# A fused diffusion block on one core: normed input for FFN 2, squares on VectorE, and a fixed distance between matmul operands

## The chip, the core and the metric

The kernel runs on one core of one Trainium2 chip. The metric is the device time of one execution in microseconds (us); smaller is better. A core has TensorE (PE in the profile; its weight loads are listed apart as PEld), VectorE (DVE), ScalarE (ACT), GpSimd (POOL) and SyncE (SP), which here issues all transfers. Each engine works through its own list of instructions in order and waits on semaphores of the others.

## The reference: what is computed

One block over 256 latent tokens and 256 context tokens, with model width 1024, in fp32:

```
x   = x   + 0.5*g1x * swiglu(modulate(rmsnorm(x), sh1x, sc1x), w13_ffn1, w2_ffn1)      # FFN 1, both streams
ctx = ctx + 0.5*g1c * swiglu(modulate(rmsnorm(ctx), sh1c, sc1c), w13_ffn1, w2_ffn1)
q,k,v,g,f,ga,gf = project(modulate(rmsnorm(...)), w_in)     # retention over 4 heads, 2-D Fourier mixing
x   = x + g2x * (sigmoid(ga)*retention_out + sigmoid(gf)*fourier) @ w_out
x   = x + 0.5*g3x * swiglu(modulate(rmsnorm(x, norm_ffn2), sh3x, sc3x), w13_ffn2, w2_ffn2)   # FFN 2, latent alone
out = rmsnorm(x, norm_final)
# rmsnorm(x, w) = x * rsqrt(mean(x*x) + eps) * w ;  modulate(h, shift, scale) = h*(1+scale) + shift
# swiglu(h, w13, w2): a, b = split(h @ w13);  (silu(a) * b) @ w2          (hidden width 2816 = 22 * 128)
```

## The kernel before

Activations lie transposed: 128 features on the partitions, tokens along the free axis, so a feature tile of the latents is 128 x 256. Every fp32 operand of a large product is held as a pair, a rounded high part and the low part that is left (names end in `h` and `l`, or the pair stands as `_0` and `_1`). `mm3` (L86) makes one product of two pairs with three matmuls into one accumulator, low weights by high input, high by low, high by high (L88, L89, L90 in every profile row). In a row such as `z<-g2h,wl` the first input is the moving operand and the second the weights. TensorE loads the weights of the following matmul while the present one streams its columns.

`load_w` (L69) fetches a weight tile with one DMA into `wr`, rounds it to `wh` on ScalarE (L78) and subtracts to `wl` on VectorE (L79; some early gate and key tiles on GpSimd). There are four buffers of each, so weights run two FFN tiles ahead.

The stages in order of time: conditioning and first products (to 66 us), FFN 1 with 512 columns (to about 400; its last two output tiles are made by stream, with 256 columns), four retention heads and the Fourier transform (`kc`, `kx`, `q`, `s`, `u`, `o`, `f`, to about 607), gates with the rest of the Fourier work (`g`, `sq`, `mx`, to 670), the merge (`gg`, `ro`, to 783), the output projection (`yo`, to 806), FFN 2 up (`fa`, `fb`, to 939), FFN 2 down (`z`, to 1003) and the final norm.

`add_sq` (L446) collects the sum of squares for a norm: ScalarE squares a feature tile into `sq` (L454), GpSimd adds it into `ssum` (L455). A matmul with a matrix of 1/1024 (`ones`) then sums over the partitions; ScalarE takes the root and VectorE the reciprocal (`rstd_of`, L222 on; the reciprocal is L228).

In FFN 2 the input `hx` is not normed: `out_proj` (L938 on) scales each feature by its column of `amul` and appends two columns, the shift vector and zeros, so a matmul streams 258 columns. Each of the 22 hidden tiles (`ffn2_up`, L966) is made with 48 matmuls (8 features, two halves `fa` and `fb`, three matmuls each); the division by the norm and the shift come afterwards, on the product: two copies of the shift columns (L978, L979), two multiplications by `rstd` (L981, L983), Silu with a bias (L982), a combined add and multiply (L984), and the split into `g2h` and `g2l`. The norm's matmul `st3` (L974) stands in the code behind the matmuls of the first hidden tile.

After the opening, which is ordered by hand, a planner sets the order of each engine's list when the kernel is built: it takes the code's instructions with its own costs and lets a matmul go ahead where it expects the operands to be there. So the order on an engine is not the order of the code.

## Time and profile before

| | |
|---|---|
| time, median of 3 runs | 1013.61 us (1013.13 to 1014.77) |
| the profiled execution: own time / span of its instructions | 1015.47 us / 1013.7 us |
| mean granted TensorE clock | 0.994 of full speed |
| PE busy, matmuls | 984.4 us (97%), x6792 |
| DVE busy | 663.9 us (65%) |
| ACT busy | 469.4 us (46%) |
| POOL busy | 62.4 us (6%), x39 |
| read from HBM | 164.70 MB, 164 GB/s over the span |

A matmul's own duration in the profile overlaps the next one's, so it tells little of the rate. What counts on a busy TensorE is the time from one start to the next, which the timeline gives. Idle time of an engine stands in brackets behind a row, with the work that ended it.

### The profile page before, as it was taken

The numbers are of one execution on the slowest core, as the hardware profiler recorded it, in microseconds if no ns is written. First come the engines' busy times: TensorE is split into PE (matmuls) and PEld (weight loads), VectorE is DVE, ScalarE is ACT, GpSimd is POOL, SyncE is SP. The second block draws the span as 40 slices with busy tenths as digits, with TensorE's granted clock in tenths as the row PEclk, the third lists the DMA queues.
The fourth block names the chain that finished last, engine by engine and source line by source line (L and its number), as shares of the span: only waits on it lengthen the run. The fifth ranks groups of instructions, "written<-read, shape, count | busy, mean of one in ns | idle before, by whom it ended". The sixth has DMA issues, their size and how long they took to land.

```text
span 1013.7 us, 16779 instructions
## 1 busy us (share of the span) xinstructions
PE 984.4 (97%) x6792; PEld 907.9 (90%) x6792; DVE 663.9 (65%) x1084; ACT 469.4 (46%) x725; POOL 62.4 (6%) x39
## 2 busy tenths in 40 slices
PE   6999999999999998999999998999999989999996
PEld 4778888888888888999999997999999989999995
DVE  7879999998334335866575538865555766676543
ACT  4454322125222423756575456754444545555541
POOL 0000000000000013000000026000000300000011
PEclk9999999999999999999999999999999999999999
DMA  8647766994322233223133434456566446656651
GB/s 337 231 176 249 235 199 212 349 402 160 104 83 75 84 112 115 64 84 125 43 126 108 158 100 150 125 185 183 181 200 187 153 161 186 185 172 182 185 174 42
DMA packets 49238, 166.84 MB, mean 165 GB/s; under 512 B 5380, under 2 KB 7044, under 8 KB 49160
## 3 DMA queue, kind: packets, MB, share of 16 engines
q1 hardware_dynamic: 49160, 165.77, 50.8%
q8 instruction: 53, 0.87, 0.3%
q14 instruction: 25, 0.20, 0.1%
HBM read 164.70 MB, written 1.05 MB: 164 GB/s over the span
## 4 chain that ended last, share of the span: by engine, by line
PE 91%; DVE 4%; ACT 2%; DMA 1%; issue 1%; POOL 0%; DVEq 0%; SPq 0%; ACTq 0%; POOLq 0%
PE y L88 4%; PE y L89 4%; PE y L90 4%; PE pa L89 3%; PE pb L89 3%; PE pa L88 3%; PE pb L88 3%; PE pb L90 3%; PE pa L90 3%; PE ro L89 2%; PE ro L90 2%; PE ro L88 2%; PE fa L89 2%; PE z L90 2%; PE z L89 2%; PE z L88 2%
## 5 line engine op out<-in xcount | busy, mean ns | idle before, releaser
L79 DVE TENSOR_TENSOR wl<-wr,wh 128x1024 fp32r<-128x1024 f32 (+1 forms) x214 | 248.8, 1164 | 202.0 <-ACT wh L78 201.2
L78 ACT CAST wh<-wr 128x1024 fp32r<-128x1024 f32 (+1 forms) x226 | 227.0, 1006 | 273.2 <-PE y L90 79.2
L191 DVE CUSTOM_DVE_ANT_0 junk<-ada,cb,sm 128x1024 bf16<-128x1024 f32 x96 | 122.9, 1280 | 5.9 <-DMA ada<-in_ada 4.4
L89 PE MATMUL y<-gl,wh 128*128 128x512 f32 (+1 forms) x198 | 72.5, 366 | 0.0
L88 PE MATMUL y<-gh,wl 128*128 128x512 f32 (+1 forms) x198 | 72.4, 366 | 0.0
L90 PE MATMUL y<-gh,wh 128*128 128x512 f32 (+1 forms) x198 | 72.3, 365 | 0.0
L455 POOL TENSOR_TENSOR ssum<-ssum,sq 128x256 f32<-128x256 f32 (+1 forms) x18 | 24.6, 1367 | 727.3 <-ACT sq L454 714.2
L89 PE MATMUL pa<-h1l,wh 128*128 128x512 f32 x152 | 59.1, 389 | 0.0
L88 PE MATMUL pa<-h1h,wl 128*128 128x512 f32 x152 | 59.1, 389 | 0.0
L90 PE MATMUL pa<-h1h,wh 128*128 128x512 f32 x152 | 59.1, 389 | 0.0
L88 PE MATMUL pb<-h1h,wl 128*128 128x512 f32 x152 | 59.1, 389 | 0.0
L89 PE MATMUL pb<-h1l,wh 128*128 128x512 f32 x152 | 59.1, 389 | 0.0
L90 PE MATMUL pb<-h1h,wh 128*128 128x512 f32 x152 | 59.1, 389 | 0.0
L89 PE MATMUL fa<-hxl,wh 128*128 128x258 f32 x176 | 50.8, 289 | 0.0
L88 PE MATMUL fa<-hxh,wl 128*128 128x258 f32 x176 | 50.8, 289 | 0.0
L90 PE MATMUL fa<-hxh,wh 128*128 128x258 f32 x176 | 50.6, 287 | 0.0
L89 PE MATMUL fb<-hxl,wh 128*128 128x258 f32 x176 | 50.1, 284 | 0.0
L89 PE MATMUL z<-g2l,wh 128*128 128x256 f32 x176 | 50.0, 284 | 0.0
L88 PE MATMUL fb<-hxh,wl 128*128 128x258 f32 x176 | 50.0, 284 | 0.0
L90 PE MATMUL fb<-hxh,wh 128*128 128x258 f32 x176 | 49.9, 283 | 0.0
L88 PE MATMUL z<-g2h,wl 128*128 128x256 f32 x176 | 49.8, 283 | 0.0
L90 PE MATMUL z<-g2h,wh 128*128 128x256 f32 x176 | 49.8, 283 | 0.0
(310 smaller groups left out, 2908.3 us busy)
## 6 DMA issues: line engine op xcount, KB each, us to landing
ada<-in_ada SPq DMA_DIRECT2D x72, 512.0 KB, 5.1
wr<-in_w13b SPq DMA_DIRECT2D x44, 512.0 KB, 4.3
wr<-in_w13a SPq DMA_DIRECT2D x38, 512.0 KB, 4.3
wrv<-in_wv SPq DMA_DIRECT2D x16, 512.0 KB, 4.3
wr<-in_wg SPq DMA_DIRECT2D x16, 512.0 KB, 4.2
wr<-in_wgate SPq DMA_DIRECT2D x16, 512.0 KB, 4.3
wr<-in_pret SPq DMA_DIRECT2D x16, 512.0 KB, 3.8
wr<-in_w2b SPq DMA_DIRECT2D x16, 512.0 KB, 3.6
```

The costliest lines, as they stand in the source:

```text
L78: S.copy(hi[:, :n], raw[:, :n])
L79: (lo_engine or V).tensor_tensor(lo[:, :n], raw[:, :n], f32(hi[:, :n]), op=ALU.subtract)
L88: PE.matmul(o, w[1], a[0], start=start, stop=False)
L89: PE.matmul(o, w[0], a[1], start=False, stop=False)
L90: PE.matmul(o, w[0], a[0], start=False, stop=stop)
L191: V.tensor_tensor_reduce(junk, raw, cb[:, s, :], 1.0, sm[:, BIAS + n : BIAS + n + 1], ALU.mult, ALU.add, mod[:, s, n : n + 1],)
L455: G.tensor_tensor(ssum[0][:, cols], ssum[0][:, cols], sq[:, :w], op=ALU.add)
```

## The change

Three things are changed.

1. FFN 2 takes a normed input from hidden tile 4 on (`RAW = 4`). Tiles 0 to 3 still use `hx` with 258 columns. While they run, `modulated` makes `hn`, the normed, scaled and shifted input, for the eight features: on VectorE one instruction for `xr`, on ScalarE one for `hnh`, on VectorE one for `hnl`. Tiles 4 to 21 stream 256 columns of `hn`; behind them stand only Silu from the accumulator, one multiplication and the split. The norm's matmul moves behind the first half of tile 1, and tiles 0 and 1 are finished together.
2. In `add_sq` the addition into `ssum` is on VectorE instead of GpSimd: five additions of 512 columns and thirteen of 256.
3. Small pads shift tiles in SBUF. Each pad is a tile that VectorE sets to zero once, nine in all, of 8 to 120 columns; `at=16` shifts some weights within their buffer, and `hx` tiles are rounded up to 288 columns.

What the third does to the layout can be told with one number for each matmul: the address of the next matmul's weights minus that of this matmul's moving operand, in bytes within 512. Here are these distances as the two built programs have them, leaving out the few matmuls at a change of stage.

| matmuls | count | before | changed |
|---|---|---|---|
| FFN 1 `pa`, `pb`, `y`, 512 columns | 1374 | 256 | 256 |
| FFN 1 last two output tiles, `y`, 256 columns | 132 | 256 | 320 |
| heads: `kc`, `kx`, `q`, `o`, and gates `g` | 1536 | 320 | 320 |
| heads: `s` and `u` | 480 | 0 | 320 |
| Fourier `f`, 512 columns | 96 | 192 | 192 |
| Fourier `sq`, `mx` | 96 | 0 | 320 |
| merge: `gg`, `ro` | 960 | 320 | 320 |
| output projection `yo` | 192 | 256 | 320 |
| FFN 2 up, tiles 0 to 3, 258 columns | 192 | sixteen values, 0 to 480 in steps of 32 | 96, 224, 352, 480 |
| FFN 2 up, tiles 4 to 21 | 864 | the same sixteen, 258 columns | 320, 256 columns |
| FFN 2 down `z` | 528 | 256 | 320 |

A distance of 320 means that the moving operand stands 192 bytes behind the weights, within 512.

The planner's order changes at three places. On PE, around the norm's matmul of FFN 2, it stood before the change between the first products of tile 0 (names end in the tile's number, then a buffer number):

```order
L88 MATMUL fa0_8180<-hxh6_7855,wl160_8190 128x258
L88 MATMUL fb0_8181<-hxh6_7855,wl160_8190 128x258
L974 MATMUL st3_8179<-ssum3_7859,ones_90 128x256
L88 MATMUL fa1_8259<-hxh0_7843,wl161_8263 128x258
L89 MATMUL fa1_8259<-hxl0_7844,wh161_8262 128x258
```

and now:

```order
L97 MATMUL fb0_8219<-hxh7_7875,wh160_8227 128x258
L96 MATMUL fa1_8280<-hxl7_7876,wh162_8289 128x258
L97 MATMUL fa1_8280<-hxh7_7875,wh162_8289 128x258
L987 MATMUL st3_8318<-ssum3_7879,ones_90 128x256
L95 MATMUL fb1_8281<-hxh0_7861,wl161_8284 128x258
L96 MATMUL fb1_8281<-hxl0_7862,wh161_8283 128x258
```

It moved from place 39 among FFN 2's matmuls to place 73, behind all of tile 0 and the first half of tile 1. It no longer stands ahead of work that could run.

On DVE, behind the norm's reciprocal in FFN 2, the weights' low parts (`wl`), the raw tiles' evacuation (`a2`) and the new `xr3` and `hnl` share the list. Before:

```order
L228 RECIPROCAL rstd3_8245<-sd3_8243 128x256
L978 COPY cc0_8247<-fa0_8180 128x1
L979 COPY cc0_8247<-fb0_8181 128x1
L981 TENSOR_TENSOR a2_0_8250<-fa0_8180,rstd3_8245 128x256
L983 TENSOR_TENSOR a2_0_8250<-fb0_8181,rstd3_8245 128x256
L978 COPY cc1_8321<-fa1_8259 128x1
L981 TENSOR_TENSOR a2_1_8324<-fa1_8259,rstd3_8245 128x256
```

and now, the last rows of the stretch, in which `hnl7` ends the making of the normed input:

```order
L328 SCALAR_TENSOR_TENSOR xr3_7_8536<-xs3_112,amul_104,rstd3_8322 128x256
L91 TENSOR_TENSOR g2l2_8459<-a2_2_8453,g2h2_8458 128x256
L1010 TENSOR_TENSOR a2_3_8543<-fa3_8462,rstd3_8322 128x256
L1012 TENSOR_TENSOR a2_3_8543<-fb3_8463,rstd3_8322 128x256
L86 TENSOR_TENSOR wl171_8694<-wr171_8692,wh171_8693 128x1024
L332 SCALAR_TENSOR_TENSOR hnl6_8215<-xr3_6_8532,mod_103,hnh6_8214 128x256
L86 TENSOR_TENSOR wl172_8700<-wr172_8698,wh172_8699 128x1024
L332 SCALAR_TENSOR_TENSOR hnl7_8217<-xr3_7_8536,mod_103,hnh7_8216 128x256
```

From the reciprocal to `hnl7`, which counts, there stand 8 `wl`, 11 TENSOR_TENSOR of 256 columns, 19 SCALAR_TENSOR_TENSOR of 256 and 5 COPY of one column. On PE the first matmul that reads `hnl0` is the 122nd behind `st3`, the first that reads `hnl7` the 232nd; tiles 4, 5 and 6 are interleaved there, by the feature that is ready. SP's list of transfers is the same in both.

The third place is where stage 2 begins, on DVE, between the last `xs` of FFN 1 and the first `h2cl`:

```order
L467 SCALAR_TENSOR_TENSOR xs3_112<-y1_7_1_3300,gate_105,xs3_112 128x256
L64 MEMSET pad_kt 128x48
L64 MEMSET pad_qt 128x80
L64 MEMSET pad_pt 128x80
L64 MEMSET pad_ht 128x48
L332 SCALAR_TENSOR_TENSOR h2cl0_3343<-xr2_0_0_3422,mod_103,h2ch0_3342 128x256
```

The four pads are new here; none of them waits for anything.

The diff:

```diff
--- before.py
+++ after.py
@@ -24,9 +24,11 @@
 M1 = 3
 HALF = MT // 2
 T2K = 4
+RAW = 4
 OUT = (P, KT, T)
 UB = 4
 HOOK = 0
+LINE = 32
 TC_KW = dict(schedule_with_timeline_sim=True)
 
 
@@ -56,6 +58,11 @@
     ada_stack = ExitStack()
     adp = fpool(ada_stack, "adp", "left")
 
+    def shifted(pool, name, eighths):
+
+        if eighths:
+            V.memset(pool.tile([P, 8 * eighths], F32, name=name), 0.0)
+
     def bank(name):
         return psum.tile([P, 512], F32, name=name, tag="ps")
 
@@ -67,16 +74,16 @@
     def wtile(t, name):
         return wp.tile([P, 1024], F32 if t == "wr" else F32R, name=name, tag=t, bufs=4)
 
-    def load_w(src, n, lo_engine=None):
+    def load_w(src, n, lo_engine=None, at=0):
 
         uid[0] += 1
-        raw, hi, lo = [wtile(t, f"{t}{uid[0]}") for t in ("wr", "wh", "wl")]
-        dst = raw[:, :n]
+        raw, hi, lo = [wtile(t, f"{t}{uid[0]}")[:, at : at + n] for t in ("wr", "wh", "wl")]
+        dst = raw
         if len(src.shape) == 3:
             dst = dst.rearrange("p (k c) -> p k c", k=src.shape[1])
         nc.sync.dma_start(dst, src)
-        S.copy(hi[:, :n], raw[:, :n])
-        (lo_engine or V).tensor_tensor(lo[:, :n], raw[:, :n], f32(hi[:, :n]), op=ALU.subtract)
+        S.copy(hi, raw)
+        (lo_engine or V).tensor_tensor(lo, raw, f32(hi), op=ALU.subtract)
         return hi, lo
 
     def split(dst_hi, dst_lo, src):
@@ -434,10 +441,10 @@
                 mm3(ps, sl(ws[k // 4], slice(None), slice(c, c + P)), h[k], k == 0, k == KT - 1)
         return gated_unit(pa, pb, f"1_{m}")
 
-    def w2_chunks(src, kts):
+    def w2_chunks(src, kts, at=0):
         ws, k0 = [], 0
         for n in kts:
-            w = load_w(src[:, k0 * P : (k0 + n) * P], n * P)
+            w = load_w(src[:, k0 * P : (k0 + n) * P], n * P, at=at)
             ws += [sl(w, slice(None), slice(c * P, (c + 1) * P)) for c in range(n)]
             k0 += n
         return ws
@@ -452,7 +459,7 @@
             S.activation(ssum[0][:, cols], ap, AF.Square)
             return
         S.activation(sq[:, :w], ap, AF.Square)
-        G.tensor_tensor(ssum[0][:, cols], ssum[0][:, cols], sq[:, :w], op=ALU.add)
+        V.tensor_tensor(ssum[0][:, cols], ssum[0][:, cols], sq[:, :w], op=ALU.add)
 
     def y_evac(ps, j, streams, st, col0):
         for n, s in enumerate(streams):
@@ -468,8 +475,9 @@
             ssum[0] = per.tile([P, 512], F32, name="ssum2", tag="ssum")
         for j in range(KT):
             some_ada(n_ada)
-            ws = w2_chunks(i["w2a"][hf, j], (6, 5))
-            if hf and j >= KT - 2:
+            in_two = hf and j >= KT - 2
+            ws = w2_chunks(i["w2a"][hf, j], (6, 5), 16 if in_two else 0)
+            if in_two:
                 late.append((j, ws))
                 continue
             ps = bank(f"y{hf}_{j}")
@@ -584,17 +592,23 @@
     ]
 
     ttp = fpool(ctx, "ttp", "left")
+    shifted(ttp, "pad_ttp", 14)
     tt = [ttp.tile([P, 512], F32, name=f"tt{n}", tag=f"tt{n}") for n in range(2 * HEADS)]
     ap = fpool(heads, "ap", "right")
     rope = ap.tile([P, 2, T], F32, name="rope")
     nc.sync.dma_start(rope, i["rope"])
     cos2, sin2 = [rope[:, n, :].unsqueeze(1).to_broadcast([P, 2, T]) for n in range(2)]
-    keys, query, sums, probs = [
-        [[ap.tile([P, 512], F32R, name=f"{nm}{n}_{x}") for x in range(2)] for n in range(cnt)]
-        for nm, cnt in (("kt", 2), ("qt", 1), ("ut", UB), ("pt", 2))
-    ]
-
-    ht = [[ap.tile([P, D], F32R, name=f"ht{t}_{x}") for x in range(2)] for t in range(4)]
+    def several(pool, nm, cnt, width, after=0):
+        tiles = [[pool.tile([P, width], F32R, name=f"{nm}{n}_{x}") for x in range(2)] for n in range(cnt)]
+        shifted(pool, f"pad_{nm}", after)
+        return tiles
+
+    keys = several(ap, "kt", 2, 512, 6)
+    query = several(ap, "qt", 1, 512, 10)
+    sums = several(ap, "ut", UB, 512, 0)
+    probs = several(ap, "pt", 2, 512, 10)
+
+    ht = several(ap, "ht", 4, D, 6)
 
     def two(a):
         return a.rearrange("p (a t) -> p a t", a=2)
@@ -766,16 +780,15 @@
             c = slice(n * 384, (n + 1) * 384)
             nc.sync.dma_start(raw[:, :384], i["dft"][:, c])
             split(dft[0][:, c], dft[1][:, c], raw[:, :384])
+        shifted(fp, "pad_dft", 10)
         fs["dft"] = dft
         for n in range(2):
             fu.append([[fp.tile([P, 512], F32R, name=f"fu{n}_{e}_{x}") for x in range(2)] for e in range(2)])
-        fs["cu"] = [
-            [fp.tile([P, 512], F32R, name=f"cu{n}_{x}") for x in range(2)] for n in range(4)
-        ]
+        shifted(fp, "pad_fu", 12)
+        fs["cu"] = several(fp, "cu", 4, 512, 10)
         mxp = fpool(mix, "mxp", "right")
-        for tiles, nm, cnt in ((mx, "mx", 4), (gt, "gt", KT)):
-            for n in range(cnt):
-                tiles.append([mxp.tile([P, 512], F32R, name=f"{nm}{n}_{x}") for x in range(2)])
+        mx.extend(several(mxp, "mx", 4, 512, 0))
+        gt.extend(several(mxp, "gt", KT, 512, 0))
 
     def sum_and_difference(p0, p1, dst, name):
         a = tp.tile([P, 512], F32, name=f"fa{name}", tag="t2k", bufs=T2K)
@@ -931,10 +944,12 @@
     V.tensor_copy(ap2[:, :, 0:1].rearrange("p k o -> p (k o)"), mod[:, 1, 6 * KT : 7 * KT])
     W = T + 2
     g2 = fpool(ctx, "g2", "left")
+    shifted(g2, "pad_g2", 15)
     hx = [
-        (g2.tile([P, W], F32R, name=f"hxh{k}"), g2.tile([P, W], F32R, name=f"hxl{k}"))
+        tuple(g2.tile([P, LINE * -(-W // LINE)], F32R, name=f"{nm}{k}")[:, :W] for nm in ("hxh", "hxl"))
         for k in range(KT)
     ]
+    shifted(g2, "pad_hx", 1)
     ssum[0] = per.tile([P, 512], F32, name="ssum3", tag="ssum")
     XC = slice(T, 2 * T)
 
@@ -960,19 +975,33 @@
     out_proj(range(6, 8))
 
 
-    ps = bank("st3")
     rstd3 = [None]
-
-    def ffn2_up(m):
-        pa, pb = bank(f"fa{m}"), bank(f"fb{m}")
+    hn_pool = fpool(ctx, "hn", "right")
+    hn = [
+        (hn_pool.tile([P, T], F32R, name=f"hnh{k}"), hn_pool.tile([P, T], F32R, name=f"hnl{k}"))
+        for k in range(KT)
+    ]
+
+    def ffn2_norm():
+        ps = bank("st3")
+        PE.matmul(ps[:, :T], ones, ssum[0][:, :T], start=True, stop=True)
+        rstd3[0] = rstd_of(ps[:, :T], T, "3")
+
+    def g2_tiles(m):
+        return [g2.tile([P, T], F32R, name=f"g2{x}{m}") for x in "hl"]
+
+    def ffn2_products(m, a, w, hook=None):
+        ps = bank(f"fa{m}"), bank(f"fb{m}")
         ws = [load_w(i["w13b"][m, n], 1024) for n in range(2)]
-        for ab, p_ in enumerate((pa, pb)):
+        for ab, p_ in enumerate(ps):
             for k in range(KT):
                 c = (k % 4) * 256 + ab * P
-                mm3(p_[:, :W], sl(ws[k // 4], slice(None), slice(c, c + P)), hx[k], k == 0, k == KT - 1)
-        if m == 0:
-            PE.matmul(ps[:, :T], ones, ssum[0][:, :T], start=True, stop=True)
-            rstd3[0] = rstd_of(ps[:, :T], T, "3")
+                mm3(p_[:, :w], sl(ws[k // 4], slice(None), slice(c, c + P)), a[k], k == 0, k == KT - 1)
+            if hook and not ab:
+                hook()
+        return ps
+
+    def raw_unit(m, pa, pb):
         r = rstd3[0]
         cc = tp.tile([P, 2], F32, name=f"cc{m}", tag="cc", bufs=4)
         V.tensor_copy(cc[:, 0:1], pa[:, T : T + 1])
@@ -982,14 +1011,27 @@
         S.activation(a[:, :T], a[:, :T], AF.Silu, bias=cc[:, 0:1])
         V.tensor_tensor(a[:, T:], pb[:, :T], r, op=ALU.mult)
         V.scalar_tensor_tensor(a[:, :T], a[:, T:], cc[:, 1:2], a[:, :T], op0=ALU.add, op1=ALU.mult)
-        gg = (
-            g2.tile([P, T], F32R, name=f"g2h{m}"),
-            g2.tile([P, T], F32R, name=f"g2l{m}"),
-        )
+        gg = g2_tiles(m)
         split(gg[0], gg[1], a[:, :T])
         return gg
 
-    g = [ffn2_up(m) for m in range(MT)]
+    def normed_unit(m):
+        pa, pb = ffn2_products(m, hn, T)
+        a = tp.tile([P, 512], F32, name=f"a2_{m}", tag="t2k", bufs=T2K)
+        S.activation(a[:, :T], pa[:, :T], AF.Silu)
+        V.tensor_tensor(a[:, :T], a[:, :T], pb[:, :T], op=ALU.mult)
+        gg = g2_tiles(m)
+        split(gg[0], gg[1], a[:, :T])
+        return gg
+
+    first = [ffn2_products(0, hx, W), ffn2_products(1, hx, W, ffn2_norm)]
+    g = [raw_unit(m, *first[m]) for m in range(2)]
+    for m in range(2, RAW):
+        pss = ffn2_products(m, hx, W)
+        for k in range((m - 2) * KT // (RAW - 2), (m - 1) * KT // (RAW - 2)):
+            modulated(hn[k], 2, (1,), k, rstd3[0], T, f"3_{k}")
+        g.append(raw_unit(m, *pss))
+    g += [normed_unit(m) for m in range(RAW, MT)]
     S.activation(warm, f32(g[MT - 1][0][:, :1]), AF.Sqrt, bias=eps, scale=0.0)
 
 
```

## The prediction

> **What bounds the kernel now.** I read the engines' shares and the chain of waits first, then the timeline of TensorE.
>
> ```profile
> PE 984.4 (97%) x6792; PEld 907.9 (90%) x6792; DVE 663.9 (65%) x1084; ACT 469.4 (46%) x725; POOL 62.4 (6%) x39
> PE 91%; DVE 4%; ACT 2%; DMA 1%; issue 1%; POOL 0%; DVEq 0%; SPq 0%; ACTq 0%; POOLq 0%
> ```
>
> 91% of the chain is TensorE itself, so a matmul that takes less time is worth its whole saving, and work on other engines is worth something only where TensorE stands waiting. How long a matmul takes is the time from start to start. These rows of TensorE's timeline (start, duration, engine, line, tiles) are ends of stretches without a stop:
>
> ```profile
> 228.38 0.39 PE L88 MATMUL pa<-h1h,wl 128*128 128x512 f32 x1
> ...
> 239.03 0.39 PE L90 MATMUL pb<-h1h,wh 128*128 128x512 f32 x1
> ...
> 481.56 0.28 PE L90 MATMUL kc<-h2ch,wh 128*128 128x256 f32 x1
> ...
> 486.32 0.28 PE L90 MATMUL kc<-h2ch,wh 128*128 128x256 f32 x1
> 486.43 0.28 PE L88 MATMUL u<-pt,ht 128*128 128x256 f32 x1
> ...
> 497.83 0.28 PE L90 MATMUL u<-pt,ht 128*128 128x256 f32 x1
> ...
> 590.32 0.40 PE L88 MATMUL f<-wh,h2xl 128*128 128x512 f32 x1
> ...
> 595.68 0.39 PE L90 MATMUL f<-wh,h2xh 128*128 128x512 f32 x1
> ...
> 596.33 0.28 PE L88 MATMUL o<-ut,wlv 128*128 128x256 f32 x1
> ...
> 612.20 0.28 PE L90 MATMUL g<-h2xh,wh 128*128 128x256 f32 x1
> ...
> 669.70 0.28 PE L88 MATMUL gg<-h2xh,wl 128*128 128x256 f32 x1
> ...
> 782.65 0.28 PE L90 MATMUL ro<-mx,wh 128*128 128x256 f32 x1
> ...
> 834.23 0.29 PE L88 MATMUL fa<-hxh,wl 128*128 128x258 f32 x1
> ...
> 939.35 0.29 PE L88 MATMUL z<-g2h,wl 128*128 128x256 f32 x1
> ...
> 994.79 0.28 PE L88 MATMUL z<-g2h,wl 128*128 128x256 f32 x1
> ```
>
> With the number of steps between two ends (counted in the code), a step takes:
> - `u`, distance 0: 11.40 us / 95 = 120.0 ns. `z`, distance 256: 55.44 / 462 = 120.0 ns.
> - `gg` and `ro`, distance 320: 112.95 / 959 = 117.8 ns.
> - `kc`, distance 320: 4.76 / 42 = 113.3 ns. `o` of head 3 from its fourth matmul and `g0`, distance 320: 15.87 / 140 = 113.4 ns.
> - FFN 2's tiles 4 to 21, 258 columns, all distances: 105.12 / 864 = 121.7 ns.
> - 512 columns: `pa`, `pb`, distance 256: 10.65 / 47 = 226.6 ns; `f`, distance 192: 5.36 / 23 = 233.0 ns.
>
> So matmuls of one width differ with the distance, which is what the change's third part sets. At 320 there are two rhythms, 117.8 and 113.4; at 0 and 256 there is only 120.0. The fast rhythm appears behind a pause, and both stretches end where matmuls of another distance follow: `u` (distance 0) starts 0.11 us behind the last `kc` and runs at 120.0. Inside a stretch of 320 nothing ends it.
>
> The other loss is one stop. The fence has five rows of TensorE's timeline, then one row of the table by windows (after the window: its length, busy time of PE, PEld, DVE, ACT and POOL with counts, granted clock, DMA share, GB/s), then one row of GpSimd's timeline:
>
> ```profile
> 810.26 0.28 PE L88 MATMUL fb<-hxh,wl 128*128 128x258 f32 x1
> 813.50 0.70 PE L974 MATMUL st<-ssum,ones 128*128 128x256 f32 x2 [2.96 <-POOL ssum L455]
> 813.85 0.47 PE L88 MATMUL fa<-hxh,wl 128*128 128x258 f32 x1
> 814.15 0.29 PE L89 MATMUL fa<-hxl,wh 128*128 128x258 f32 x1
> ...
> 819.63 0.29 PE L88 MATMUL fb<-hxh,wl 128*128 128x258 f32 x1
> 814.41:817.82 3.41, 3.41 (x18) 3.41 (x17) 1.75 (x1) 0.30 (x1) 0.00 (x0) 0.50 0.27 107
> 808.50 4.95 POOL L455 TENSOR_TENSOR ssum<-ssum,sq 128x256 f32<-128x256 f32 x2 [3.35 <-ACT sq L454]
> ```
>
> The norm's matmul waits for GpSimd's last two additions. Then the window row (the 0.50 is the granted clock) shows 3.41 us at half clock, begun 0.9 us after the stop.
>
> **The change part by part.** (1) The stop. From 810.26 to 819.63 are 9.37 us. In them run 35 products (24 of `fa1`, 5 of `fa0`, 6 of `fb0`) and the norm's matmul: 35 x 0.1217 + 0.35 = 4.6 us. Now `st3` stands 34 matmuls later, about 4 us, and the additions are on VectorE. Its rows there:
>
> ```profile
> 796.96 1.30 DVE L84 TENSOR_TENSOR hxl<-xa,hxh 128x258 fp32r<-128x258 f32 x2
> 799.31 0.96 DVE L84 TENSOR_TENSOR hxl<-xa,hxh 128x258 fp32r<-128x258 f32 x1
> 806.17 0.43 DVE L84 TENSOR_TENSOR hxl<-xa,hxh 128x258 fp32r<-128x258 f32 x1
> 807.90 2.35 DVE L79 TENSOR_TENSOR wl<-wr,wh 128x1024 fp32r<-128x1024 f32 x2
> 810.17 0.76 DVE L84 TENSOR_TENSOR hxl<-xa,hxh 128x258 fp32r<-128x258 f32 x2
> 814.74 1.75 DVE L228 RECIPROCAL rstd<-sd 128x256 f32<-128x256 f32 x1 [2.68 <-ACT sd L226]
> ```
>
> An addition there should cost what an `hxl` of 258 columns does alone, 0.43 us; seven are 3.0 us. Beside a running GpSimd addition one `hxl` took 0.96, so about 2 us come back over the stage. VectorE ended `hxl7` at 810.93; one `wl` and two additions more make it about 813, and the row at 810.26 is the place just ahead of `st3` before; 34 products later it is due at about 810.26 + 35 x 0.122 = 814.5. No stop, then, and no half clock; a matmul with `ones` still leaves a gap behind it (813.85 to 814.15, 0.30 instead of 0.12). Saved: 9.37 - 4.61 - 0.2 = **4.5 us**. Bounds: 0 if `st3` still waits, 4.8.
>
> (2) Columns and distance of FFN 2's tiles 4 to 21: 864 matmuls from 121.7 to 117.8 ns: **3.4 us**. Bounds: at 120.0, 1.5; at 113.4, 7.2.
>
> (3) Distance 320 for `u`, `s`, `yo`, `z` and the late `y`: 384 + 96 + 192 + 528 + 132 = 1332 matmuls from 120.0 to 117.8: **2.9 us**. Bounds: none, and 8.8 at 113.4. `sq` and `mx` lie between stops and count nothing here. The raw tiles 0 to 3 (192 matmuls) get four of the sixteen distances they had; between 120.0 and 125 that is 0.6 us either way, and I take none.
>
> (4) The hand-over to `hn`. VectorE's list from the reciprocal to `hnl7` has 8 `wl`, 11 small TENSOR_TENSOR, 19 SCALAR_TENSOR_TENSOR and 5 copies. The groups by line give their durations (`xr` and `h1l` of FFN 1 are the same forms):
>
> ```profile
> L79 DVE TENSOR_TENSOR wl<-wr,wh 128x1024 fp32r<-128x1024 f32 x174 | 212.7, 1223 | 163.0 <-ACT wh L78 162.4
> L364 DVE SCALAR_TENSOR_TENSOR xr<-xs,amul,rstd 128x256 f32<-128x256 f32 x16 | 7.1, 482 | 0.4
> L84 DVE TENSOR_TENSOR g2l<-a,g2h 128x256 fp32r<-128x256 f32 x22 | 9.2, 416 | 0.1
> L979 DVE COPY cc<-fb 128x1 f32<-128x1 f32 x22 | 3.4, 153 | 0.4 <-PE fb L90 0.4
> L118 DVE MEMSET ones<- 128x128 f32 x1 | 0.2, 165 | 0.0
> ```
>
> 8 x 1.22 + 11 x 0.42 + 19 x 0.48 + 5 x 0.15 = 24.2 us at most, since neighbours overlap a little; with the 3.0 us from `st3`'s start to the reciprocal's end (813.50 to 816.49) 27.2. TensorE has 232 matmuls before it needs `hnl7`: 120 x 0.1217 + 112 x 0.1178 + 0.5 = 28.3 us. `hnl0` is needed after 122, far later than it is made. So it is hidden, by a microsecond at the worst and by some 4 with the overlap. If that cover goes, the matmuls of tiles 4 to 6 wait for it, and a half-clock stretch may follow. Later VectorE has four instructions fewer for each tile.
>
> (5) Pads: a memset of 128 columns took 0.165 us. Four stand ahead of stage 2's first `h2cl`, which TensorE waits for: **0.3 us lost** (0 to 0.7). The others run beside full queues of TensorE.
>
> So far 4.5 + 3.4 + 2.9 - 0.3 = 10.5 us.
>
> (6) The fast rhythm. With one distance for everything, nothing shown in this trace ends it once it has begun. It begins at `kc` of head 2 (481.56), behind the norm matmul's pause, and the `u`, `q`, `o`, `s`, `kx` behind it no longer change the distance: 192 + 96 + 192 + 48 + 48 = 576 matmuls of heads 1 to 3; then `u` of head 3 (96, behind the same kind of pause); it held in `o` and `g0`; behind the Fourier stops it would hold through `g3` to `g7` with `mx` (276), `gg`, `ro` (960) and `yo` (192). That is 2100 matmuls x (117.8 - 113.4 = 4.4 ns) = **9.3 us**. Bounds: 0, and 6.1 more if FFN 2's 864 and the 528 `z` run fast too. There the raw tiles' other distances come first, and at other distances the rhythm was lost; so I take 117.8 for these.
>
> The Trainium skill, "TensorE: Matmul & The Clock Gate", section "Step-by-step: what each phase is for", says that TensorE has two independent SBUF read ports, so that loading the next weights takes nothing from the running matmul; by that, distance is worth nothing. Its section "Back-to-back issue gap" gives N/2.4 + 2.5 ns, an estimate of 109.2 for 256 columns, and 0.8 ns for two columns. The trace has 113.4, 117.8 and 120.0 for the same 256 columns and does not agree.
>
> Sum on the profiled execution's own 1015.47 us: 1015.47 - 10.5 - 9.3 = 995.7. The median of the runs stands at 1013.61 / 1015.47 of it: **994 us**.
>
> **The rivals.**
> - *Slow rhythm throughout.* The 117.8 of `gg` is what 320 gives, and the short fast stretches end by themselves: term (6) is nothing. For it: 959 steps at 117.8 that never turned fast. Against: `o` and `g0` held 140 steps over many tile boundaries. 1015.47 - 10.5 = 1005.0, 1003 us as a median.
> - *Fast to the end.* FFN 2 and `z` too: 6.1 us more, 988 us. For it: the hand-over may bring short pauses at distance 320, and pauses are where the rhythm began. Against: the raw tiles.
> - *Distance is worth nothing.* The steps belong to the stages (`u` and `z` are other tiles than `gg`), as the page's rule has it. Then the stop's 4.5 us stay and two columns of 258, 0.94 ns x 864 = 0.8 us, less 0.3: 1009 us. Against: `u` and `z` agree at 120.0 though they are quite different stages.
> - *The hand-over stops TensorE.* VectorE's 27 us get longer than the cover by the 4 us that the overlap was worth, and 1.5 us go at half clock (3.41 x 0.5, rounded down): 999 us.
> - *Slower: 192 bytes apart costs.* `f`, the one stage with weights 192 bytes behind the moving operand, is the slowest of its width, 233.0 against 226.6. If a gap of 192 bytes costs 6.4 ns in either direction, the 1332 + 864 matmuls lose 14.1 us against the 5.0 that are left in "distance is worth nothing" (4.5 + 0.8 - 0.3): 1015.47 + 14.1 - 5.0 = 1024.6, 1023 us as a median. It decides from 5.0 / 2196 = 2.3 ns a matmul. Against: `gg` at 320 is below 120.
>
> That the change does not do what it says is not one: in the built program all but some 40 of the 256-column matmuls have distance 320.
>
> **How the numbers follow.** Forecast 0.42; fast to the end 0.23; slow throughout 0.23; hand-over stop 0.05; distance worth nothing 0.04; slower 0.03. The range from 986 to 1005 holds the first four cases with their unknown ends (some 0.85 of the chance after errors of size). This kernel's runs tell apart about 0.2%, 2 us: faster 0.95, same 0.02, slower 0.03.
>
> **What would show it.** Right: no idle time before `st`, clock 1.0 there; `u` and `z` below 118 ns a step; `gg` and `ro` at 113.4. Wrong: `gg` and `ro` still at 117.8 (forecast too low by up to 9); `fa` of tiles 4 to 21 at 113.4 (too high by 6); idle time before `fa` with `hn`; `z` at 120 or more, which would end the whole reading of distances.

## The result, and the profile after

The changed kernel takes 987.79 us (median of 4 runs, 986.11 to 988.43); the kernel before took 1013.84 us beside it (4 runs, 1013.13 to 1014.77). The ratio is 0.9744, with a 95% interval from 0.9731 to 0.9757: 26 us less. The profiled execution took 986.11 us, with a span of 984.3 us at a mean granted clock of 0.995. The first two rows are the engines' shares and the chain of waits on the page of the changed kernel.

```profile
PE 957.3 (97%) x6792; PEld 881.2 (90%) x6792; DVE 658.1 (67%) x1056; ACT 468.1 (48%) x733; POOL 37.7 (4%) x21
PE 93%; DVE 3%; ACT 1%; DMA 1%; issue 1%; DVEq 0%; SPq 0%; ACTq 0%
```

TensorE has as many instructions as before, is as busy by share, and carries 93% of the chain instead of 91%. So the same matmuls got shorter. The table cuts TensorE's timeline at the first start of a stage; the end is the last start of `z`, and the times are us.

| stage | before | changed |
|---|---|---|
| opening, to the first `pa` behind it | 66.7 | 63.4 |
| FFN 1, to the first `kc` | 333.4 | 333.2 |
| heads, Fourier, gates, merge, projection, to the first `fa` | 405.7 | 395.5 |
| FFN 2 up, to the first `z` | 133.6 | 121.5 |
| FFN 2 down, to the last `z` | 63.7 | 60.2 |
| final norm and output | 10.7 | 10.6 |

The opening's 3.3 us are not the change's: over the twelve profiles of this study its length lies between 63.4 and 66.8 us, without regard to what was changed. Behind the opening the two profiles differ by 946.9 - 920.9 = 26.0 us, which is what the medians of the runs differ by (26.05). So the stages behind it can be compared from profile to profile, but for one place. Where stage 2 begins (first `kc`), the granted clock is halved in every profile: for 3.41 us in five of them, before and changed among these, and for 6.83 us in seven. One row each of the table by windows, of the changed kernel and of one with 6.83 us (behind the window its length, then the busy times and counts of PE, PEld, DVE, ACT and POOL, the granted clock, DMA share and GB/s):

```profile
400.77:404.18 3.41, 3.41 (x17) 3.05 (x16) 3.41 (x4) 0.75 (x2) 2.47 (x1) 0.50 0.10 40
400.38:407.20 6.82, 6.27 (x26) 5.54 (x27) 6.82 (x16) 3.98 (x9) 2.48 (x1) 0.50 0.46 139
```

From the first `kc` to the first `q` the five take 22.9 to 23.4 us and the seven 23.9 to 24.4. The kernel with the short matmuls in `z`, whose instructions there are those of the changed kernel, is one of the seven. So up to 1 us in the stage from `kc` to `yo` is no edit's; it is named below where it matters.

These rows of TensorE's timeline are ends of stretches, as in the prediction:

```profile
482.27 0.28 PE L95 MATMUL u<-pt,ht 128*128 128x256 f32 x1
...
493.04 0.28 PE L97 MATMUL u<-pt,ht 128*128 128x256 f32 x1
...
661.02 0.28 PE L95 MATMUL gg<-h2xh,wl 128*128 128x256 f32 x1
...
769.71 0.28 PE L97 MATMUL ro<-mx,wh 128*128 128x256 f32 x1
...
780.68 0.19 PEld L95 LDWEIGHTS yo<-mg,wl 128*128 128x128 f32 x1
780.71 0.35 PE L95 MATMUL yo<-mg,wl 128*128 128x256 f32 x1
780.90 0.28 PE L96 MATMUL yo<-mg,wh 128*128 128x256 f32 x1
...
791.97 0.28 PE L97 MATMUL yo<-mg,wh 128*128 128x256 f32 x1
...
816.20 0.28 PE L97 MATMUL fa<-hnh,wh 128*128 128x256 f32 x1
...
913.44 0.28 PE L97 MATMUL fb<-hnh,wh 128*128 128x256 f32 x1
913.55 0.28 PE L95 MATMUL z<-g2h,wl 128*128 128x256 f32 x1
...
969.65 0.28 PE L95 MATMUL z<-g2h,wl 128*128 128x256 f32 x1
```

By steps: `u` of head 1 10.77 us / 95 = 113.4 ns (120.0 before); `gg` and `ro` 108.69 / 959 = 113.3 (117.8 before); the tiles with `hn` 97.24 / 858 = 113.3 (121.7 before); `z` 56.10 / 495 = 113.3 (120.0 before). The fast rhythm runs through FFN 2 and `z` to the end. It is not everywhere: the step behind 780.71 took 0.19 us, since the weights of that matmul came late (their load, the row of PEld, starts 0.03 us ahead of the matmul; in the fast stretches it is 0.11), and from there `yo` ran at 11.07 / 94 = 117.8.

At the norm of FFN 2 there is no stop any more. Three rows of TensorE's timeline, one row of the table by windows (1.00 is the granted clock), one row of VectorE's timeline that ends the making of `hn`, and the row of TensorE in which `hnl7` is first read:

```profile
800.65 0.28 PE L97 MATMUL fa<-hxh,wh 128*128 128x258 f32 x1
800.77 0.60 PE L987 MATMUL st<-ssum,ones 128*128 128x256 f32 x2
801.02 0.47 PE L95 MATMUL fb<-hxh,wl 128*128 128x258 f32 x1
...
800.80:804.20 3.40, 3.40 (x29) 3.34 (x28) 2.64 (x4) 2.41 (x3) 0.00 (x0) 1.00 0.32 114
...
824.74 0.49 DVE L332 SCALAR_TENSOR_TENSOR hnl<-xr,mod,hnh 128x256 fp32r<-128x256 f32 x1
...
828.10 0.39 PE L96 MATMUL fa<-hnl,wh 128*128 128x256 f32 x2
```

`st3` follows 0.12 us behind its neighbour, and the clock stays at 1.00. `hnl7` ends at 825.23, 3 us before it is read.

### The profile page after: what moved, and what is told of

Read it like the earlier page. It is cut to its first block, busy times and chain, and to the rows that moved or that the text cites. A ratio compares the mean times of both kernels' runs of the same rounds, so it can differ in the third digit from the quotient of the medians.

```text
span 984.3 us, 16732 instructions
## 1 busy us (share of the span) xinstructions
PE 957.3 (97%) x6792; PEld 881.2 (90%) x6792; DVE 658.1 (67%) x1056; ACT 468.1 (48%) x733; POOL 37.7 (4%) x21
## 3 DMA queue, kind: packets, MB, share of 16 engines
HBM read 164.70 MB, written 1.05 MB: 168 GB/s over the span
## 4 chain that ended last, share of the span: by engine, by line
PE 93%; DVE 3%; ACT 1%; DMA 1%; issue 1%; DVEq 0%; SPq 0%; ACTq 0%
PE y L95 4%; PE y L97 4%; PE y L96 4%; PE pa L97 4%; PE pb L95 4%; PE pa L95 4%; PE pb L97 4%; PE pa L96 3%; PE pb L96 3%; PE ro L97 2%; PE ro L95 2%; PE ro L96 2%; PE fb L97 2%; PE fa L97 2%; PE fb L96 2%; PE fa L96 2%
## 5 line engine op out<-in xcount | busy, mean ns | idle before, releaser
L86 POOL TENSOR_TENSOR wl<-wr,wh 128x1024 fp32r<-128x1024 f32 x12 | 29.9, 2515 | 439.2 <-ACT wh L85 439.2
L96 PEld LDWEIGHTS y<-gl,wh 128*128 128x128 f32 x198 | 37.3, 188 | 6.1
L95 PEld LDWEIGHTS y<-gh,wl 128*128 128x128 f32 x198 | 37.2, 188 | 6.0
L97 PEld LDWEIGHTS y<-gh,wh 128*128 128x128 f32 x198 | 37.2, 188 | 6.0
L97 PE MATMUL fb<-hnh,wh 128*128 128x256 f32 x144 | 39.8, 276 | 0.0
L96 PE MATMUL fb<-hnl,wh 128*128 128x256 f32 x144 | 39.8, 276 | 0.0
L97 PE MATMUL fa<-hnh,wh 128*128 128x256 f32 x144 | 39.8, 276 | 0.0
```

The lines of the kernel that those rows point to most:

```text
L86: (lo_engine or V).tensor_tensor(lo, raw, f32(hi), op=ALU.subtract)
L95: PE.matmul(o, w[1], a[0], start=start, stop=False)
L96: PE.matmul(o, w[0], a[1], start=False, stop=False)
L97: PE.matmul(o, w[0], a[0], start=False, stop=stop)
```

## The experiments

The kernel before was timed anew beside each group of kernels (medians 1013.28, 1014.12 and 1013.88), and each ratio is to the runs beside it. Kernels that differ by less than about 2 us in the runs are compared by their stages behind the opening.

### The layout alone

The kernel before, with all pads, `at=16` and `hx` of 288 columns:

```diff
+    shifted(ttp, "pad_ttp", 14)
 ...
+            ws = w2_chunks(i["w2a"][hf, j], (6, 5), 16 if in_two else 0)
 ...
+    shifted(g2, "pad_g2", 15)
```

> The kernel before with the third part of the change alone (pads, shifted weights, hx tiles of 288 columns); FFN 2 stays unnormed in all 22 tiles and GpSimd keeps the additions. Theory 'distance': stages from the first kc to the last yo shrink as in the changed kernel (405.7 us before, 395.5 there: 10.2 us), z goes from 120.0 to 113.3 ns (3.5 us) or to 117.8 (1.2 us), the 1056 matmuls of 258 columns from 121.7 to 120.5 (1.2 us); the stop ahead of st3 stays. Sum 12.6 to 14.9 us: 999 to 1001 us. Rival 'columns' (distance is worth nothing, all gain is from the normed input and the additions): 1013.8 to 1014.2 us, z at 120.0 ns.

1001.97 us (4 runs, 998.63 to 1002.62), ratio 0.9880 (0.9854 to 0.9907). The stages from `kc` to `yo` took 396.8 us and `z` 60.2 us, nearly the changed kernel's 395.5 and 60.2 (0.7 of the 1.3 us lie between the first `kc` and the first `q`, where this profile has the half clock for 6.83 us). "Columns" falls: most of the gain in these stages comes with the layout alone, and `z` is fast with unnormed tiles in front of it. FFN 2 up took 132.1 us (133.6 before), its matmuls of 258 columns 120.0 ns instead of 121.7. The stop stayed, and was a little longer. From TensorE's timeline and the table by windows of this kernel:

```profile
801.32 0.28 PE L95 MATMUL fb<-hxh,wl 128*128 128x258 f32 x1
804.89 1.22 PE L1027 MATMUL st<-ssum,ones 128*128 128x256 f32 x2 [3.29 <-POOL ssum L462]
...
804.62:808.03 3.41, 3.14 (x12) 2.97 (x13) 1.38 (x1) 0.47 (x1) 0.21 (x1) 0.50 0.57 204
```

By the stages behind the opening this kernel gained 13.9 us, inside the expected 12.6 to 14.9; the runs' median says 11.3. The opening of this profile is the longest of all (66.8 us); whether the runs' openings explain the rest isn't known, since one execution of each kernel has a profile.

### Everything but the layout

```diff
-        if eighths:
+        if eighths and False:
 ...
-LINE = 32
+LINE = 1
 ...
-            ws = w2_chunks(i["w2a"][hf, j], (6, 5), 16 if in_two else 0)
+            ws = w2_chunks(i["w2a"][hf, j], (6, 5), 0)
```

> The changed kernel without its third part: no pads, no shifted weights, hx tiles of 258 columns. The normed tiles of FFN 2 still happen to lie at distance 320 (864 matmuls), z is at 256 again, u and s at 0, yo at 256. Theory 'distance': FFN 2's tiles 4 to 21 run at 113.3 ns (864 x 8.4 = 7.3 us) and the stop is gone (4.5 us), z stays at 120.0: 1002 us; at 117.8 in FFN 2 1006 us. Rival 'columns': nothing is lost against the changed kernel, 988 us, z at 113.3.

1001.96 us (1001.26 to 1003.67), ratio 0.9891 (0.9873 to 0.9908); expected 1002. FFN 2 up took 121.6 us as in the changed kernel: here too its 864 matmuls happen to lie at 320 and ran at 113.3 ns, although the raw tiles ahead of them had all sixteen distances. `z`, at 256, took 63.6 us as before. From `kc` to `yo` it took 406.7 us (405.7 before; the 1.0 lies at the half clock, 6.83 us here), so nothing of that stage's gain is left. Behind the opening this kernel gained 11.0 us; with the 13.9 of the layout alone that is 24.9 of the 26.0. So `z`'s gain is the layout's and FFN 2's is the normed input's, which took the extra columns and the foreign distances away in one. The view of one tile shows the rhythm in another way. Its columns are duration in ns (least, median, most) and first and last start; the first two rows are `z` of this kernel, the next two `z` of the changed one:

```profile
L96 PEld LDWEIGHTS z<-g2l,wh x176: 187/192/193, 926.0 to 989.4; 128*128 128x128 f32 x176
L97 PE MATMUL z<-g2h,wh x176: 278/283/284, 926.2 to 989.6; 128*128 128x256 f32 x176
```

```profile
L96 PEld LDWEIGHTS z<-g2l,wh x176: 187/188/190, 913.6 to 973.5; 128*128 128x128 f32 x176
L97 PE MATMUL z<-g2h,wh x176: 276/276/283, 913.8 to 973.7; 128*128 128x256 f32 x176
```

At distance 256 a weight load takes 192 ns instead of 188, and the matmul 283 instead of 276: 7 ns, the difference of the steps 120.0 and 113.3. (The ends of matmuls are modelled in the profile, so the 7 ns are no second measurement of the step.)

### The additions alone

```diff
-        G.tensor_tensor(ssum[0][:, cols], ssum[0][:, cols], sq[:, :w], op=ALU.add)
+        V.tensor_tensor(ssum[0][:, cols], ssum[0][:, cols], sq[:, :w], op=ALU.add)
```

> The kernel before with one line changed: the addition into ssum is on VectorE. The planner now puts st3 behind all of tile 0. Theory 'the additions made the stop': no idle time ahead of st3, no half clock behind it, 4.5 us less: 1009.3 us; all steps elsewhere as before. Rival 'VectorE becomes late instead': VectorE's list holds the last additions back, and 1 to 2 us of the stop stay with the half clock: 1011 to 1012 us. Rival 'GpSimd's traffic made the slow rhythm': gg and ro turn to 113.3 ns (960 x 4.4 = 4.2 us), 1005 us.

1010.75 us (10 runs, 1009.47 to 1012.17), ratio 0.9976 (0.9966 to 0.9986), between the first two expectations. FFN 2 up took 130.2 us, 3.4 less than before and 1.1 short of the 4.5. `st3` itself no longer waits, and no half clock follows, but VectorE's list now holds two `hxl` back:

```profile
807.33 0.28 PE L88 MATMUL fb<-hxh,wl 128*128 128x258 f32 x1
807.98 0.39 PE L89 MATMUL fa<-hxl,wh 128*128 128x258 f32 x1 [0.37 <-DVE hxl L84]
...
810.13 0.39 PE L89 MATMUL fa<-hxl,wh 128*128 128x258 f32 x1 [0.45 <-DVE hxl L84]
...
810.72 0.59 PE L974 MATMUL st<-ssum,ones 128*128 128x256 f32 x2
...
809.50:813.00 3.50, 3.05 (x24) 2.82 (x23) 2.22 (x6) 1.42 (x2) 0.00 (x0) 1.00 0.84 247
```

The edit is not the engine alone: the planner also put `st3` ten matmuls later, behind all of tile 0. But there, 7.12 us behind the first `fa`, it would have had to wait if GpSimd had done them, since before the change GpSimd's last addition ended 7.65 us behind the first `fa`; VectorE's ended at 6.80. By this reckoning GpSimd's lateness is what made the stop, at the old place and at this one, and a piece of it came back as VectorE's lateness, as the second expectation had it, but without its half clock. `gg` and `ro` stayed at 117.8 ns, so GpSimd's traffic is not what makes the rhythm.

### The additions back on GpSimd

The changed kernel with that line undone.

> The changed kernel with the additions into ssum back on GpSimd; st3 keeps its place behind the first half of tile 1. Theory 'moving st3 was enough': GpSimd's last addition lands about a microsecond ahead of st3, no stop, 988 us as the changed kernel. Rival 'VectorE was needed': VectorE's instructions take longer beside GpSimd's additions (0.96 instead of 0.43 us was one hxl) and st3 or an hxl stops TensorE by 1 to 3 us with a half-clock stretch behind: 990 to 992 us.

988.20 us (987.49 to 989.50), ratio 0.9748 (0.9733 to 0.9762): no difference from the changed kernel that can be measured, and FFN 2 up takes 121.5 us as there. GpSimd's last two additions and `st3`, from the two engines' timelines:

```profile
796.81 4.98 POOL L462 TENSOR_TENSOR ssum<-ssum,sq 128x256 f32<-128x256 f32 x2 [3.35 <-ACT sq L461]
...
802.06 0.59 PE L987 MATMUL st<-ssum,ones 128*128 128x256 f32 x2
```

GpSimd ends at 801.79, 0.27 us ahead of `st3`. Moving `st3` behind work that can run was what removed the stop; with it moved, the squares on VectorE are worth nothing that shows.

### Three raw tiles instead of four

```diff
-RAW = 4
+RAW = 3
```

> The changed kernel with three raw tiles instead of four (RAW = 3). hnl7 is then read first 153 matmuls behind st3 instead of 232. TensorE covers 153 x 0.118 + 0.5 = 18.5 us; VectorE needs 3.9 us from st3's start to the reciprocal's end as in the changed kernel, then 5 wl, 8 additions and products, 18 SCALAR_TENSOR_TENSOR and 3 copies: 18.6 us by single durations, 15.8 with the overlap that the changed kernel showed (20.5 us there for 24.2). Theory 'the cover just held': about 1.3 us of waits at the first tiles of 256 columns, perhaps a half-clock stretch behind them, 48 matmuls 7 ns shorter: 988.5 to 990.5 us. Rival 'the hand-over is far from late': no wait, 987.5 us.

991.87 us (990.32 to 997.39), ratio 0.9801 (0.9771 to 0.9830), slower than the changed kernel. FFN 2 up took 123.4 us (121.5 there). The stops are where they were expected, 1.7 us in all instead of 1.3:

```profile
812.19 0.28 PE L95 MATMUL fb<-hnh,wl 128*128 128x256 f32 x1
812.63 0.38 PE L96 MATMUL fa<-hnl,wh 128*128 128x256 f32 x1 [0.16 <-DVE hnl L332]
...
816.04 0.28 PE L95 MATMUL fb<-hnh,wl 128*128 128x256 f32 x1
817.22 0.38 PE L96 MATMUL fa<-hnl,wh 128*128 128x256 f32 x1 [0.90 <-DVE hnl L332]
...
817.40:820.80 3.40, 3.40 (x29) 3.27 (x29) 3.40 (x10) 2.38 (x5) 0.00 (x0) 1.00 0.36 123
```

The steps of 0.44 and 1.18 us in place of 0.11, with another of 0.44 for a `wl`, are 1.7 us too long; five more of 0.21 to 0.22 us, most of them right behind such a step, add 0.5. The 48 matmuls that are now 7 ns shorter give 0.3 back, which makes the 1.9 us of the stage. So the fourth raw tile is what covers the hand-over. Another 1.2 us lie in the stage ahead (396.7 us against 395.5; 0.6 of it at the half clock, 6.83 us here), which the edit doesn't touch, and 1.0 in the opening.

### A row of distances

The changed kernel, with another offset of the weights for each output tile of FFN 1, and for five hidden tiles of each `z`:

```diff
-            ws = w2_chunks(i["w2a"][hf, j], (6, 5), 16 if in_two else 0)
+            ws = w2_chunks(i["w2a"][hf, j], (6, 5), 16 if in_two else 16 * j + 8 * hf)
 ...
-        ws = w2_chunks(i["w2b"][j], (8, 8, 6))
+        ws = z_chunks(i["w2b"][j], (6, 5, 6, 5), 16 * j)      # the offset in the second chunk alone
```

> The changed kernel with FFN 1's down projection at fifteen distances, one for each output tile (512 columns, 33 matmuls each: 256 to 192 in steps of 64 in the first half, 288 to 32 in steps of 64 in the second), and with five of the 22 hidden tiles of each z output at another distance (256 columns, 15 matmuls: 384, 448, 0, 64, 128, 192, 256), the rest at 320. Theory 'distance': the step depends on the distance in both widths: 512 columns 226.7 ns at 256, 233 at 192, below 226.7 near 320; z 120.0 at 0 and 256, 113.3 to 117.8 at 320, behind each foreign stretch the rhythm is chosen anew. Rival 'sign does not matter': 192 and 320 give the same step. Rival 'columns': all steps of one width agree.

994.43 us (one run). Mean steps in ns between the matmuls of a stretch, from the starts in TensorE's timeline; the last column is the rhythm of the `z` matmuls at 320 behind each foreign stretch.

| distance | `y`, 512 columns | `z`, 256 columns | then at 320 |
|---|---|---|---|
| 0 | 227.0 | 119.9 | 117.8 |
| 64 | 233.3 | 117.8 | 117.8 |
| 128 | 232.2 | 118.9 | 113.3 |
| 192 | 229.2 | 113.4 | 113.3 |
| 256 | 226.9 | 120.0 | 117.8 |
| 320 | 233.2 | 113.3 or 117.8 | |
| 384 | 232.6 | 117.9 | 117.8 |
| 448 | 228.9 | 117.7 | 113.3 |

The six odd multiples of 32 that were tried (288 to 480, 32, 96) lie between 233.1 and 234.3 with 512 columns. "Distance" is right in both widths, but against my expectation the two widths do not want the same distances: with 512 columns 0 and 256 are the best, which with 256 columns are the worst, and 320, where I expected less than 226.7, costs 6.5 ns more. FFN 1 is right where it lies. With 256 columns 192 is as good as 320 (15 matmuls in a fast surrounding), so "the sign does not matter" is right for these two. In `z` it was the weights that moved here; between the kernel without the layout and the changed one it was `g2`. At 256 both come out at 120.0, so the difference of the two addresses counts and not the place of one operand. The last column says that a foreign stretch can change the rhythm of what follows: 0, 256 and 384 were entered fast and left slow, 128 and 448 entered slow and left fast (each was tried once). And a distance need not have one step with 512 columns either: `f`, at 192 in every kernel, ran at 233.4 ns before and at 229.2 and 228.9 in the changed kernel.

### Short matmuls as a disturbance

In `z` of the changed kernel, 15 times, an extra matmul of n columns at distance 320, with its weights there in time:

```diff
             mm3(py[:, :T], ws[k], g[k], k == 0, k == MT - 1)
+            if k in (4, 14) and (j or k == 14):
+                n = 32 * j + (16 if k == 14 else 0)
+                PE.matmul(kick[:, :n], ws[k][1], g[k][0][:, :n], start=True, stop=True)
```

> The changed kernel with fifteen short extra matmuls in z (g2h moving, wl as weights, distance 320 like all others, into an unused PSUM bank), of 16, 32, ... 240 columns, 30 to 36 ordinary matmuls apart; z alone tells. Theory 'phase': the rhythm hangs on when a weight load falls within the running matmul, and a short matmul shifts it; behind some widths z goes on at 117.8 ns, behind others at 113.3, and each holds until the next. Rival 'foreign distance or late weights only': at one distance and with the weights in time nothing ends the fast rhythm, all fifteen stretches stay at 113.3.

991.04 us (one run). "Phase" is right. From TensorE's timeline, the first, the second, the fourth and the fifth extra matmul (`kick`):

```profile
920.54 0.17 PE L1049 MATMUL kick<-g2h,wl 128*128 128x16 f32 x1
...
920.77 0.28 PE L96 MATMUL z<-g2l,wh 128*128 128x256 f32 x1
...
924.89 0.18 PE L1049 MATMUL kick<-g2h,wl 128*128 128x32 f32 x1
...
932.89 0.20 PE L1049 MATMUL kick<-g2h,wl 128*128 128x64 f32 x1
...
933.48 0.28 PE L96 MATMUL z<-g2l,wh 128*128 128x256 f32 x1
...
936.42 0.20 PE L1049 MATMUL kick<-g2h,wl 128*128 128x80 f32 x1
```

Behind 16 columns `z` goes on at (924.89 - 920.77) / 35 = 117.7 ns, behind 64 at (936.42 - 933.48) / 26 = 113.1; over the whole second half of that stretch the mean is 113.3. Behind 16, 32, 48, 80, 96, 128, 160, 176 and 240 columns the rhythm was slow, behind 64, 112, 144, 192, 208 and 224 fast, and each held until the next extra matmul. Each width was tried once, from the rhythm that the one ahead had left: 16, 80, 128, 160 and 240 ended a fast stretch, 64, 112, 144 and 192 a slow one, the others changed nothing. No foreign distance and no other stage is in it. A late step is, behind the narrow ones: behind 16 columns the second step is 0.20 us. But behind 240 columns no step is above 0.122 us, and the rhythm is slow from there on:

```profile
976.18 0.27 PE L1049 MATMUL kick<-g2h,wl 128*128 128x240 f32 x1
976.29 0.28 PE L95 MATMUL z<-g2h,wl 128*128 128x256 f32 x1
```

So both rhythms are states of the same stream, and a disturbance of tens of ns can switch between them. Each `kick` costs about 0.12 us by itself.

### The crossings of the heads

In the changed kernel the slow stretches of heads begin where a matmul at distance 0 or 128 stands between two stages. Moving one pad gives `s` crossings at 320:

```diff
+    shifted(ap, "pad_rope", 10)
     keys = several(ap, "kt", 2, 512, 6)
-    query = several(ap, "qt", 1, 512, 10)
+    query = several(ap, "qt", 1, 512, 0)
```

> The changed kernel with one pad moved: 320 bytes stand ahead of the key tiles instead of behind the query tile, so keys and query lie 192 bytes lower and the matmuls at the ends of s (o to s at 0, s to the next at 128) have distance 320 too. Theory 'an odd distance at a crossing ends the fast rhythm': s, kc1, u0, q1, o0, kx2 and kx3, 435 matmuls now at 117.8 ns, run at 113.3: 1.9 us less, 986 us. Rival 'the stages choose': s and what follows stay at 117.8, 988 us.

989.64 us (989.08 to 993.13), ratio 0.9768 (0.9750 to 0.9785); not the 986 expected. The theory was right at its place and wrong in the sum. From TensorE's timeline:

```profile
422.62 0.28 PE L95 MATMUL q<-h2xh,wl 128*128 128x256 f32 x1
...
476.57 0.28 PE L97 MATMUL kx<-h2xh,wh 128*128 128x256 f32 x1
476.69 1.03 PE L767 MATMUL ov<-os,ones_dv 128*128 128x256 f32 x4
...
477.91 0.28 PE L95 MATMUL kc<-h2ch,wl 128*128 128x256 f32 x1
...
518.42 0.28 PE L97 MATMUL kx<-h2xh,wh 128*128 128x256 f32 x1
```

From `q0` through `s`, `kc1`, `u`, `q1`, `o` and `kx2` it is one fast stretch, 53.95 us / 476 = 113.3 ns, where the changed kernel had some 350 of these at 117.8 (1.57 us more for the same matmuls). But behind the norm's matmuls `ov`, which in the changed kernel were entered slow and left fast, this kernel was entered fast and left slow: (518.42 - 477.91) / 344 = 117.8. The next `ov` was entered slow and left slow, so the rhythm ahead of a pause does not by itself decide the one behind it. The stage from `kc` to `yo` got 2.0 us longer (397.5 against 395.5), 0.9 of it at the half clock (6.83 us here).

Two more kernels add one extra matmul, of 64 or of 112 columns, in the first tile behind each of the three pauses:

```diff
+    def nudge(o, w, a):
+        PE.matmul(o[:, :64], w[1], a[0][:, :64], start=True, stop=True)
 ...
+                if nudged and (e, k) == (1, 0):
+                    nudge(o, w, a[k])
```

> The kernel with the keys and query at 192 bytes lower (run before this one: 476 matmuls from q0 to kx2 in one fast stretch, but kc2, kc3 and u3 came slow out of the pauses ahead of them: 359 + 310 + 94 matmuls at 117.8 ns), with one extra matmul of 64 columns in the middle of the first tile behind each of the three pauses, where 64 columns turned z from slow to fast. Theory 'phase': all three stretches turn to 113.3 ns behind the extra matmul; 700 x 4.4 = 3.1 us less, 3 x 0.12 us more: 2.7 us below that kernel in the stages from kc to o, 987 us. Rival 'where in the slow rhythm's period of three it falls decides too': some of the three stay slow; each that stays costs up to 1.5 us.

> The same with 112 columns in place of 64; 112 also turned z from slow to fast. Theory 'phase': as with 64. Rival 'period of three': 64 and 112 need not do the same here as in z.

With 64 columns: 988.37 us (987.49 to 990.30), ratio 0.9753 (0.9736 to 0.9769). `kc2` and `kc3` turned fast, 330 and 283 matmuls in one stretch each; `u3` did not. The stage from `kc` to `yo` took 395.1 us, the shortest of all, 2.4 us below the kernel without it (397.5). 2.7 were expected, but 1.05 of the 2.4 is the half clock, which lasts 3.41 us here and 6.83 there. From the first `q` to the first `f`, which holds the two stretches that turned, this kernel is 2.5 us shorter (606 x 4.4 ns less two extra matmuls); behind that it loses 1.1. With 112 columns: 989.67 us (988.15 to 991.20), ratio 0.9759 (0.9743 to 0.9775). `kc2` and `u3` turned, `kc3` did not, and `q0`, far ahead of any edit, began slow this time and stayed so for 479 matmuls. So a width that turned `z` does not turn every stage: what else decides, the place in the slow rhythm's period of three or something before it, was not told apart. Where nothing ahead differs the rhythms mostly repeat: from the first `q` to the first `f` the changed kernel takes 134.43 us, and the five other kernels whose heads are the same take 134.41 to 134.42. Neither kernel beats the changed one by more than can be measured.

## Why the prediction was right, and where it was not

The time lies in the range, and the gain is 26.05 us where I forecast 19.8. The likeliest case did not come; the rival "fast to the end", 0.23 and 988 us, did, by its time and by where the fast rhythm ran. Its reason did not: it counted on short pauses at the hand-over, and there were none. The first matmul that reads `hn` in the changed kernel is

```profile
815.61 0.28 PE L95 MATMUL fa<-hnh,wl 128*128 128x256 f32 x1
```

and from there to 816.20 five steps take 0.59 us, none above 0.124; then it is 113.3. What makes the stream settle in the fast rhythm at that crossing is not shown. So the rival's number was right without its mechanism. By the steps of the prediction:

- **(1) The stop: 4.5 us, right.** FFN 2 up lost 12.1 us. 864 x (121.7 - 113.3) ns are 7.3, the raw tiles at 120.3 instead of 121.7 some 0.2, and 4.6 are left. That the new place of `st3` is enough for this is shown by the kernel with the additions back on GpSimd. I had put both edits to one account; the additions, with `st3` ten matmuls later, brought 3.4 of it.
- **(2) FFN 2's tiles 4 to 21: 3.4 us forecast, 7.3 measured.** This is the step that failed. I took 117.8, because the raw tiles ahead have other distances and I had seen the fast rhythm lost at such. That the raw tiles are not fast is right (they ran at 120.3); that what follows must be slow is not. It was fast behind them in all nine kernels in which these tiles lie at 320, with sixteen foreign distances or with four.
- **(3) `z`: 1.2 us of the 2.9 forecast, 3.5 measured,** for the same reason. It follows FFN 2 without a change of distance. These two make 3.9 + 2.3 = 6.2 us, as much as the whole miss; the other terms miss by less than 1 us each and cancel.
- **(4) The hand-over: hidden, right,** and by 3 us where I had said one at the worst and some 4 with the overlap. With three raw tiles it is no longer hidden.
- **(5) The pads: 0.3 us forecast, 0.25 measured, right.** TensorE's wait for the first `h2cl`, in the kernel without the layout and in the one with the additions back on GpSimd, whose clocks are alike there (between the two starts around it are 0.64 us in the three kernels without the four pads and 0.89 in the nine with them):

```profile
401.13 0.58 PE L96 MATMUL kc<-h2cl,wh 128*128 128x256 f32 x1 [0.27 <-DVE h2cl L332]
401.10 0.58 PE L96 MATMUL kc<-h2cl,wh 128*128 128x256 f32 x1 [0.52 <-DVE h2cl L332]
```

- **(3) for the late `y`: 0.3 us forecast, 0.4 measured** (16.98 us before, 16.57 now), of which 0.2 reach the first `kc`.
- **(3) for `u`, `s` and `yo`, with (6), the fast rhythm up to `yo`: 1.5 + 9.3 us forecast, 10.2 measured, but not where I said.** (2100 x 4.4 ns are 9.2, not 9.3.) Of the 2100 I had counted, `s`, `kx` of head 3, `mx` and the second half of `yo` stayed slow, and `o` of head 3 and `g0`, fast before, turned slow (142 matmuls, 0.6 us lost). In exchange there was a little in other places, 0.4 us of it in `f`, whose distance the change leaves alone. The sum is closer than its parts deserve.
- **"Nothing ends it once it has begun" is wrong as I put it.** One late load of weights (780.71), one crossing at another distance, one short matmul can end it, and can begin it too. The reading that a pause begins it was half of this: behind `ov` the stream came out fast in the changed kernel and slow in the one with the keys moved.

The Trainium skill, "TensorE: Matmul & The Clock Gate", section "Step-by-step: what each phase is for", would have had distance worth nothing, as the prediction reads it. The two kernels with half the change each do not agree: with the layout alone `z` goes from 120.0 to 113.3 ns, without it it stays at 120.0. The section "Back-to-back issue gap" of the same page of the Trainium skill calls its N/2.4 + 2.5 ns the gap of a single matmul by itself and says that in a stream the weight loads set the spacing too; the 109.2 ns that the prediction took from it was therefore no figure for this stream.

"Slower: 192 bytes apart costs" was drawn from `f`, with 512 columns. The row of distances shows that 512 columns do want 0 or 256, and that this must not be carried to 256 columns. And `f` at the same distance is 229 ns in the changed kernel, so its 233.0 was not the distance's alone.

## What to carry to other kernels

Where TensorE bounds a kernel, take the step from start to start of one form of matmul in each stage; if it has several values, look at where weights and moving operand lie within 512 bytes before looking at anything that waits. In the view of one tile the median of the weight loads (188 or 192 ns here) and of the matmuls (276, 281 or 283) tells the rhythm in one row. Find the best distance for each width by itself, and put a matmul that waits behind work that can run before making what it waits for faster. The same distance at the crossings between stages made one long stretch fast here, but no kernel faster. Before two profiles are compared by a stage, see whether the clock was halved in it for equally long.
